# The q and k projections of two head groups by seven block products instead of eight, with v and the attended heads kept in DRAM

## The chip, the cores and the metric

One core of a Trainium2 chip runs the whole program. The metric is the device time of one execution in microseconds (us). The engines are named as in the profile: PE (TensorE matmul), PEld (its weight loads), DVE (VectorE), ACT (ScalarE), POOL (GpSimd, whose queue also issues some DMAs), SP (SyncE, which issues most loads). Each engine works through its own list of instructions in order.

## The reference

One layer of an encoder with 512 positions and 1024 channels, everything in float32:

```python
n = rms_norm(h, norm_mix_pre)
proj = n @ w_in                      # columns: u, v of the gMLP | q | k | v of attention | gates
z_gmlp, q, k, v, gates = split(proj)
y_a = u * (W_s LN(v) + b_s)          # chunked gMLP gating
q, k = partial_rope(q), partial_rope(k)          # 12 heads of 128: 3 groups of 4
for g, (window, dilation) in enumerate(((128, 1), (512, 4), (2048, 16))):
    o_g, lse_g = dilated_window_attention(q_g, k_g, v_g, dilation, ...)
y_b = sum(softmax(lse over groups) * o_g)        # 4 heads of 128
merged = sigmoid(g_a) * (y_a @ w_branch_a) + sigmoid(g_b) * (y_b @ w_branch_b)
h = h + rms_norm(merged @ w_out)
h = h + rms_norm(relu(rms_norm(h) @ w_up) ** 2 @ w_down)
```

## The kernel before, in words

Each float32 operand of a large product is split into two parts, a rounded `hi` and the rest `lo`: ACT copies to `hi`, DVE subtracts to get `lo` (`wsplit`, lines 74 and 75, for weights; `split_into`, lines 79 and 80). A product is then three matmuls, hi·hi, hi·lo and lo·hi (`mm3`, lines 84 to 86).

The stages in order of time: norm of x and the first v group; v of the two other groups (`token_major`); the q/k stage, head by head; the gMLP's v and u with head 3's attention between them (the u stage); gates and branches; w_out; up projection; down projection. `n` is kept transposed as `nh`, `nl` (128 partitions x 8 blocks x 512 positions) for the first five.

*The q/k stage* (`project_qk`) loads for each head and each of three groups one `qkw` tile (q and k weights, 512 KB together, issued by SP), splits each half, and makes q and k with one `feature_tile` each: 8 blocks x 3 matmuls of 512 columns. ACT evacuates the accumulator twice, 32 rows into `st` for the rotary step and all rows into the tile. `rotate` (lines 311 to 316) turns `st` on DVE and ACT writes it back; `split_qk` and `scores_a` make scores of group 0 (psa), `scores_b` those of groups 1 and 2 (psb); `softmax_tile` and `mix` finish the probabilities. `attend(h - 1)` runs between groups 1 and 2 of head h; head 3's runs in pieces inside the u stage. `v0h`, `v0l` and `v12` (v of all heads, 32 KB in each partition) and `ybh`, `ybl` (the attended heads, split) stay on chip throughout.

*The seven-product scheme* is already used in the gate stage (`seven`, `product`, `seven_pairs`, lines 548 to 596) and in another form in the up projection. Two output tiles of 128 columns over 512 positions are a 2 x 2 block problem: channels even/odd, positions in halves `A` and `B` of 256. Instead of eight block products there are seven, numbered 1 to 7, each 4 blocks x 3 matmuls of 256 columns. They need sums of weight blocks (tile `s`, three DVE instructions, `seven`) and sums of blocks of n. These four sums are made once by `four_sums` after the second v group, stored to DRAM (`sums`), and loaded again before the gate stage (tiles `nt`, line 635, POOL queue). Three accumulators Y, Z, X are shared by the seven products, so snapshots have to be taken between them:

```python
product(6, Y, ...)
product(1, X, ...)
nc.scalar.activation(p1, X, AF.Copy)                       # L578
nc.vector.tensor_tensor(u2, Y, p1, op=ALU.add)             # L579
product(5, Z, ...)
nc.scalar.activation(z5, Z, AF.Copy)                       # L581
product(2, X, ...); evac(i, c1[:, A], X)
product(7, Y, ...)
nc.vector.scalar_tensor_tensor(u3, Y, -1.0, p1, ...)       # L585
product(3, Z, ...)
nc.vector.tensor_tensor(c1[:, B], Z, u2, op=ALU.add)       # L587
nc.vector.tensor_tensor(c2[:, B], u3, z5, op=ALU.subtract) # L588
```

Product 4, into Y, and the last quarter (`c2[:, A]`, L592) are held back in `tail` and issued after product 6 of the next pair.

The order of instructions on each engine is set when the program is built, by a scheduler that works through the code above by its own estimate of time; pools with a number of buffers (`bufs`) say how far a producer may run ahead. Weights come from `wpool` (`raw`, `hi` and `lo` with three buffers each), accumulators from `psA` (tag `acc` four buffers, `S` two, `T` and `y` one).

Of the kernel before, what the change touches and what calls it, by code (L numbers as in the profile page):

```python
# [10 lines left out]
F32 = mybir.dt.float32  # L11
# [5 lines left out]
P = 128  # L17
# [19 lines left out]
def block_kernel(ctx: ExitStack, tc: tile.TileContext, x, norm_mix_pre, w_in, b_gate, ln_v_gain, ln_v_bias,  # L37
# [70 lines left out]

    front = ExitStack()
# [101 lines left out]
    for i in range(4):  # L211
        if i + 1 < 4:
            _, hi, lo = norm_x(blocks[i + 1], xts[i + 1], rs[i + 1])
        if i == 0:
            with tc.issue_after(hi.ins):
                for j in (2, 3):
                    rs[j], _ = square_x(blocks[j], xts[j])
        b = blocks[i]
        pv = psA.tile([P, GW], F32, name="pv", tag="acc", bufs=4)
        for k in range(KD):  # L220
            sl = slice(b * P, (b + 1) * P)
            mm3(pv, (nh[:, k, sl], nl[:, k, sl]), w0[k], k == 0, k == KD - 1)
        split_into(v0h[:, b], v0l[:, b], pv)
    start.close()

    carry = pool(right, "carry", side="right")
    ybh = carry.tile([P, NH, S], F32R, name="ybh")
    ybl = carry.tile([P, NH, S], F32R, name="ybl")
# [22 lines left out]
    sums = {n: tc.dram_tile([P, 2, KH, 256], F32R, name=f"sum{n}") for n in (6, 5, 7, 4)}  # L251

    def four_sums():
        with ExitStack() as st:
            spool = pool(st, "spool")
            f = spool.tile([P, KD, S], F32, name="nf")
# [12 lines left out]
    for g in range(2):  # L269
        def ev(r, ps, g=g):  # L270
            if r % 2:
                nc.vector.tensor_copy(v12[:, g, r], ps)
            else:
                nc.scalar.activation(v12[:, g, r], ps, AF.Copy)
        with tc.issue_after(hi.ins), tc.issue_after(lo.ins):
            token_major(COL_VV + (g + 1) * GW, lambda n, k, r: n[:, k, ROT + r:ROT + S:4], ev)
        if g == 0:
            four_sums()

# [9 lines left out]
    ppool = pool(attn, "ppool", bufs=16)  # L289
# [17 lines left out]

    def rotate(st, tiles, r0):
# [9 lines left out]
    def project_qk(h):  # L318
        got, tiles, r0 = {}, [], 0
        st = apool.tile([P, S], F32, name="st", bufs=2)  # L320
        for g in range(3):
            if g == 2:
                st, tiles, r0 = apool.tile([P, S], F32, name="st", bufs=2), [], 64
                if h:
                    attend(h - 1)
            hd0 = (g * NH + h) * HD
            raw = wload([2, KD, P], lambda r: [(r[:, 0], fcols(w_in, COL_Q + hd0, KD, P)), (r[:, 1], fcols(w_in, COL_K + hd0, KD, P))], "qkw")
            for j, nm in enumerate("qk"):
                wh, wl = wsplit(raw[:, j])
                ps = feature_tile(wh, wl, KD, nhn, nln)  # L330
                d = apool.tile([P, S], F32, name=f"{nm}{g}")
                view = ps.rearrange("p (l r) -> p r l", r=4) if g else ps
                i = r0 + 32 * len(tiles)
                for dst, src in ((st[i:i + 32], view[0:32]), (d, view)):
                    nc.scalar.activation(dst.rearrange("p (r l) -> p r l", r=4) if g else dst, src, AF.Copy)
                tiles.append(d)
                got[nm, g] = d.rearrange("p (r l) -> p r l", r=4)
# [64 lines left out]
    def mix(h):  # L402
# [4 lines left out]
        pp = psA.tile(shape, F32, name="pp", tag="T")  # L407
# [22 lines left out]
        pc = psA.tile(sq, F32, name="pc", tag="T")  # L430
# [14 lines left out]
    def attend_steps(h, tag="T", nb=1):  # L445
        hs = slice(h * HD, (h + 1) * HD)
# [30 lines left out]
        for k in range(4):  # L477
# [7 lines left out]
            a = (v0h[:, k, hs], v0l[:, k, hs])  # L485
# [6 lines left out]
        for r in range(4):  # L492
            o = py[:, r:S:4]
            for g in range(2):
                nc.tensor.matmul(o, v12[:, g, r, hs], ptb[r // 2][:, r % 2, g], start=False,  # L495
                                 stop=(r == 3 and g == 1), skip_group_check=True)
        split_into(ybh[:, h], ybl[:, h], py)
# [5 lines left out]

    yapool = pool(right, "yapool", side="right")
# [43 lines left out]
    def seven(raw, sums, split2, split1):  # L548
        raw = raw.rearrange("p (j h) (r c) -> p j (h r) c", h=2, r=2)
        s = sums()  # L550
        nc.vector.tensor_tensor(s[:, :, 0:4:2], raw[:, :, 1:3], raw[:, :, 0:1].to_broadcast([P, KH, 2, P]), op=ALU.add)
        nc.vector.tensor_tensor(s[:, :, 3], s[:, :, 2], raw[:, :, 1], op=ALU.add)
        s12 = split2(s[:, :, 2:4])
        ar = [split1(raw[:, :, 1], "ar0"), split1(raw[:, :, 2], "ar1")]
        a12 = split1(raw[:, :, 3], "a12")
        nc.vector.tensor_tensor(s[:, :, 1], s[:, :, 3], raw[:, :, 3], op=ALU.add)
        s34 = split2(s[:, :, 0:2])
        pick = lambda g, i: [z[:, :, i] for z in g]
        return {1: ar[0], 2: a12, 3: pick(s34, 1), 4: ar[1], 5: pick(s12, 0), 6: pick(s12, 1), 7: pick(s34, 0)}

    def product(n, ps, w, moving, first):
        (wh, wl), (bh, bl) = w[n], moving[n]
        for j in range(KH):
            for i, (a, b) in enumerate(((wh, bh), (wh, bl), (wl, bh))):
                nc.tensor.matmul(ps, a[:, j], b[:, j], start=first and not (j or i), stop=(j == KH - 1 and i == 2), skip_group_check=True)  # L565

    def seven_pairs(n, weights, moving, banks, snap, two, rows, evac, after):
        tail = None
        for i in range(n):
            c2, c1 = rows(i)  # L570
            w = weights(i)
            Y, Z, X = banks()
            product(6, Y, w, moving, True)
            if tail:
                tail()
            product(1, X, w, moving, True)
            p1, z5, u2, u3 = snap("p1", two), snap("z5", 1), snap("u2", 1), snap("u3", 1)
            nc.scalar.activation(p1, X, AF.Copy)  # L578
            nc.vector.tensor_tensor(u2, Y, p1, op=ALU.add)  # L579
            product(5, Z, w, moving, True)  # L580
            nc.scalar.activation(z5, Z, AF.Copy)  # L581
            product(2, X, w, moving, False)
            evac(i, c1[:, A], X)
            product(7, Y, w, moving, False)
            nc.vector.scalar_tensor_tensor(u3, Y, -1.0, p1, op0=ALU.mult, op1=ALU.subtract)  # L585
            product(3, Z, w, moving, False)
            nc.vector.tensor_tensor(c1[:, B], Z, u2, op=ALU.add)  # L587
            nc.vector.tensor_tensor(c2[:, B], u3, z5, op=ALU.subtract)  # L588

            def tail(i=i, w=w, Y=Y, p1=p1, c2=c2):  # L590
                product(4, Y, w, moving, False)
                nc.vector.scalar_tensor_tensor(c2[:, A], Y, -1.0, p1, op0=ALU.mult, op1=ALU.subtract)  # L592
                after(i)
        tail()

    steps = attend_steps(NH - 1, "S", 2)
    next(steps)
    for g2 in range(2):
        raw = wload([KD, 2 * P], lambda r: [(r, fcols(w_in, COL_U + g2 * 2 * P, KD, 2 * P))], "uw")
        for j in range(2):  # L600
# [17 lines left out]
            t = gpool.tile([P, 4, P], F32, name="sv", bufs=2)  # L618
# [11 lines left out]
    spacer(gp, 32, "tedge", "left")  # L630
    tpool = pool(gp, "tpool", bufs=4)
    nmov = {}
    for n in (6, 5, 7, 4):
        hl = tpool.tile([P, 2, KH, 256], F32R, name="nt")
        nc.gpsimd.dma_start(hl, sums[n])
        nmov[n] = (hl[:, 0], hl[:, 1])
    gst.close()
    spacer(gp, 224, "gedge", "left")
# [18 lines left out]
    def gate_weights(i):  # L657
        raw = gate_raw(i + GSTD)

        def split1(src, tag):  # L660
            hl = gapool.tile([P, 2, KH, P], F32R, name=tag)
            split_into(hl[:, 0], hl[:, 1], src)
            return hl[:, 0], hl[:, 1]

        return seven(raw.rearrange("p k r c -> p k (r c)"), lambda: wpool.tile([P, KH, 4, P], F32, name="s", tag="raw"), wsplit, split1)
# [25 lines left out]
    for d in range(GSTD):  # L691
# [5 lines left out]
        if d == 0:  # L697
            for n, (kh, half) in {1: (0, A), 2: (1, A), 3: (1, B)}.items():
                nmov[n] = (nhn[:, kh:KD:2, half], nln[:, kh:KD:2, half])
# [323 lines left out]
```

## Time and profile before

| | |
|---|---|
| median of 3 executions | 814.74 us (814.69 to 815.55) |
| the profiled execution, whole | 814.79 us |
| its span, first to last instruction | 813.0 us |
| granted TensorE clock | 0.998 |
| busy PE / PEld / DVE / ACT / POOL | 801.5 / 711.2 / 493.4 / 413.2 / 43.7 us |
| moved by DMA | 95.73 MB |

How to read the views. The page gives busy time by engine. The view of waits has "engine line waited for: us in total, times, longest". The view of stretches gives, for a piece of the span, its length, then busy time and number of instructions of each engine, the clock, the DMA engines' share and GB/s. The groups of instructions give "line engine op out<-in forms xcount | busy us, mean ns | idle before them <- releaser". The chain in order of time gives "start, us, engine, tile, line, count", and the timeline "start, us, engine, line, instruction". DMA issues give size in KB and median us from issue to landing. Buffer numbers are left out of names: `pf` is a feature tile's accumulator, `pgacc` and `pgS` those of the gate stage, `pacc` and `ptp` those of the up projection.

### The profile page before, as it was taken

The numbers are of one execution on the slowest core, as the hardware profiler recorded it, in microseconds if no ns is written. First come the engines' busy times: TensorE is split into PE (matmuls) and PEld (weight loads), VectorE is DVE, ScalarE is ACT, GpSimd is POOL, SyncE is SP. The second block draws the span as 40 slices with busy tenths as digits, with TensorE's granted clock in tenths as the row PEclk, the third lists the DMA queues.
The fourth block names the chain that finished last, engine by engine and source line by source line (L and its number), as shares of the span: only waits on it lengthen the run. The fifth ranks groups of instructions, "written<-read, shape, count | busy, mean of one in ns | idle before, by whom it ended". The sixth has DMA issues, their size and how long they took to land.

```text
span 813.0 us, 11561 instructions
## 1 busy us (share of the span) xinstructions
PE 801.5 (99%) x4629; PEld 711.2 (87%) x4629; DVE 493.4 (61%) x827; ACT 413.2 (51%) x689; POOL 43.7 (5%) x69
## 2 busy tenths in 40 slices
PE   8999999999999999999999999999999999999996
PEld 5899888888888889999988899999999888888885
DVE  6762264646463978788656479988887533333324
ACT  6341367666665555454535447666676522332212
POOL 3012000000002400000001100000000000000000
PEclk9999999999999999999999999999999999999999
DMA  9377333131312463344447222333334632332202
GB/s 309 109 242 204 87 103 104 53 102 54 97 60 65 127 209 105 79 117 118 130 140 246 80 79 87 121 105 104 105 108 144 233 112 103 104 103 75 82 1 104
DMA packets 84056, 95.73 MB, mean 118 GB/s; under 512 B 2417, under 2 KB 70033, under 8 KB 82978
## 3 DMA queue, kind: packets, MB, share of 16 engines
q1 hardware_dynamic: 80208, 77.60, 31.5%
q0 software_dynamic: 3792, 17.39, 6.2%
q8 instruction: 36, 0.59, 0.3%
q14 instruction: 18, 0.15, 0.1%
q10 hardware_dynamic: 2, 0.00, 0.0%
HBM read 86.60 MB, written 8.39 MB: 117 GB/s over the span
## 4 chain that ended last, share of the span: by engine, by line
PE 93%; DVE 3%; DMA 1%; ACT 1%; issue 0%; DVEq 0%; POOLq 0%; POOL 0%; ACTq 0%
PE pacc L890 11%; PE pd L84 9%; PE pd L85 9%; PE pd L86 9%; PE pf L85 9%; PE pf L84 9%; PE pf L86 9%; PE pgacc L565 6%; PE ptp L890 4%; PE pv L85 3%; PE pv L86 3%; PE pv L84 3%; PE pgS L565 2%; PE psb L383 1%; PE py L495 1%; DMA upw<-in_w_up_dram 1%
## 5 line engine op out<-in xcount | busy, mean ns | idle before, releaser
L84 PE MATMUL pf<-nh,hi 128*128 128x512 f32 x240 | 94.7, 395 | 0.0
L86 PE MATMUL pf<-nh,lo 128*128 128x512 f32 x240 | 94.4, 393 | 0.0
L85 PE MATMUL pf<-nl,hi 128*128 128x512 f32 x240 | 94.2, 393 | 0.0
L85 PE MATMUL pd<-hl,hh 128*128 128x512 f32 x224 | 87.2, 390 | 0.0
L84 PE MATMUL pd<-hl,hh 128*128 128x512 f32 x224 | 86.3, 389 | 0.0
L86 PE MATMUL pd<-hl 128*128 128x512 f32 x224 | 86.1, 389 | 0.0
L890 PE MATMUL pacc<-nt,hl 128*128 128x256 f32 x504 | 67.6, 280 | 0.1
L80 DVE TENSOR_TENSOR hl<-hid,hh 128x512 fp32r<-128x512 f32 x28 | 19.2, 692 | 75.6 <-ACT hh L79 75.6
L75 DVE TENSOR_TENSOR lo<-qkw,hi 128x1024 fp32r<-128x1024 f32 x24 | 29.4, 1226 | 57.7 <-ACT hi L74 57.7
L890 PEld LDWEIGHTS pacc<-nt,hl 128*128 128x128 f32 x504 | 62.7, 188 | 0.3 <-ACT hl L79 0.3
L79 ACT ACTIVATE hh<-hid 128x512 fp32r<-128x512 f32 x28 | 17.4, 630 | 89.0 <-PE pd L85 89.0
L86 PEld LDWEIGHTS pf<-nh,lo 128*128 128x128 f32 x240 | 45.1, 188 | 9.1
L85 PEld LDWEIGHTS pf<-nl,hi 128*128 128x128 f32 x240 | 45.2, 188 | 8.9
L84 PEld LDWEIGHTS pf<-nh,hi 128*128 128x128 f32 x240 | 45.2, 188 | 8.6
L86 PEld LDWEIGHTS pd<-hl 128*128 128x128 f32 x224 | 42.1, 188 | 8.7
L85 PEld LDWEIGHTS pd<-hl,hh 128*128 128x128 f32 x224 | 42.1, 188 | 8.6
L84 PEld LDWEIGHTS pd<-hl,hh 128*128 128x128 f32 x224 | 42.0, 188 | 8.6
L80 DVE TENSOR_TENSOR hl<-dnw,hl 128x1024 fp32r<-128x1024 f32 x32 | 39.1, 1225 | 13.9 <-ACT hl L79 13.9
L890 PE MATMUL pacc<-n,hl 128*128 128x256 f32 x336 | 45.2, 280 | 0.5 <-ACT z L915 0.5
L79 ACT ACTIVATE hl<-s 128x1024 fp32r<-128x1024 f32 x28 | 29.6, 1058 | 28.9 <-DVE s L874 10.6
L890 PEld LDWEIGHTS pacc<-n,hl 128*128 128x128 f32 x336 | 41.9, 188 | 0.8 <-ACT z L915 0.7
L79 ACT ACTIVATE hl<-dnw 128x1024 fp32r<-128x1024 f32 x32 | 33.4, 1048 | 12.4 <-PE pacc L890 7.5
(315 smaller groups left out, 1930.5 us busy)
## 6 DMA issues: line engine op xcount, KB each, us to landing
upw<-in_w_up_dram SPq DMA_DIRECT2D x16, 1024.0 KB, 5.5
dnw<-in_w_down_dram SPq DMA_DIRECT2D x16, 1024.0 KB, 4.9
qkw<-in_w_in_dram SPq DMA_DIRECT2D x24, 512.0 KB, 5.3
gw<-in_w_in_dram SPq DMA_DIRECT2D x16, 512.0 KB, 5.2
slab<-in_w_in_dram SPq DMA_DIRECT2D x6, 1024.0 KB, 9.2
sum<-sum POOLq DMA_DIRECT2D x4, 1024.0 KB, 7.8
nt<-sum POOLq DMA_DIRECT2D x4, 1024.0 KB, 7.5
wow<-in_w_out_dram SPq DMA_DIRECT2D x4, 1024.0 KB, 5.1
```

Source lines behind the costliest of these rows:

```text
L75: (sub or nc.vector).tensor_tensor(lo, raw, hi.bitcast(F32), op=ALU.subtract)
L79: nc.scalar.activation(hi, src, AF.Copy)
L80: return nc.vector.tensor_tensor(lo, src, hi.bitcast(F32), op=ALU.subtract)
L84: nc.tensor.matmul(ps, ah, bh, start=start, stop=False)
L85: nc.tensor.matmul(ps, ah, bl, start=False, stop=False)
L86: return nc.tensor.matmul(ps, al, bh, start=False, stop=stop)
L383: nc.tensor.matmul(ps[:, rr, g - 1], got["q", g][:, r], got["k", g][:, r], start=True, stop=True)
L495: nc.tensor.matmul(o, v12[:, g, r, hs], ptb[r // 2][:, r % 2, g], start=False, stop=(r == 3 and g == 1), skip_group_check=True)
L565: nc.tensor.matmul(ps, a[:, j], b[:, j], start=first and not (j or i), stop=(j == KH - 1 and i == 2), skip_group_check=True)
L890: nc.tensor.matmul(ps, a[:, j], b[:, j], start=first and not (j or m), stop=(j == KH - 1 and m == 2), skip_group_check=True)
```

## The change

q and k of groups 0 and 1 of every head are made as one pair by the seven-product scheme (`seven_qk`); group 2's two tiles stay with `feature_tile`. The four sums of n go straight into tiles `nmov` that stay on chip to the end of the gate stage (32 KB a partition); they are no longer stored and loaded. To make room v is split or copied into staging tiles and stored to DRAM by POOL's queue (`v0d`, `v12d`), and each head's part is loaded before it is needed into one buffer (`load_v`: for head 0 at the start, for the others after `attend(h - 1)`). The attended heads 0 to 2 are stored (`ybd`) and loaded together after the q/k stage; head 3's is written in place. Smaller: `ppool` has 15 buffers instead of 16, `sv` one instead of two, head 3's `mix` uses the accumulators tagged `S`.

```diff
+    spool = pool(right, "spool", bufs=4, side="right")
+    nmov = {n: spool.tile([P, 2, KD // 2, 256], F32R, name="nt") for n in (6, 5, 7, 4)}
...
-    vpool = pool(attn, "vpool")
-    v0h = vpool.tile([P, 4, GW], F32R, name="v0h")
-    v0l = vpool.tile([P, 4, GW], F32R, name="v0l")
-    v12 = vpool.tile([P, 2, 4, GW], F32, name="v12")
+    vtmp = pool(vst, "vtmp")
+    v0d = tc.dram_tile([P, 2, 4, GW], F32R, name="v0d")
+    v12d = tc.dram_tile([P, 2, 4, GW], F32, name="v12d")
+    ybd = tc.dram_tile([P, NH - 1, 2, S], F32R, name="ybd")
...
-        split_into(v0h[:, b], v0l[:, b], pv)
+        t = vtmp.tile([P, 2, GW], F32R, name="v0", bufs=2)
+        split_into(t[:, 0], t[:, 1], pv)
+        nc.gpsimd.dma_start(v0d[:, :, b], t)
...
-                hl = spool.tile([P, 2, KH, 256], F32R, name="sum", bufs=4)
+                hl = nmov[n]
                 split_into(hl[:, 0], hl[:, 1], part)
-                nc.gpsimd.dma_start(sums[n], hl)
...
+            t = vtmp.tile([P, GW], F32, name="v12", bufs=4)
...
+            nc.gpsimd.dma_start(v12d[:, g, r], t)
...
+    def load_v(h):
+        hs = slice(h * HD, (h + 1) * HD)
+        v0, v12 = vpool.tile([P, 2, 4, HD], F32R, name="v0s"), vpool.tile([P, 2, 4, HD], F32, name="v12s")
+        for src, dst in ((v0d, v0), (v12d, v12)):
+            nc.gpsimd.dma_start(dst.rearrange("p a b c -> p (a b) c"), src[:, :, :, hs].rearrange("p a b c -> p (a b) c"))
+        heads[h] = v0, v12
...
+    qkpool = pool(proj, "qkpool")
...
+    def seven_qk(raw, g, c2, c1):
+        w = seven(raw.rearrange("p k r c -> p k (r c)"), wsum, wsplit, split1)
+        Y, Z, X = [psA.tile([P, 512], F32, name="pg", tag="acc", bufs=4)[:, A] for _ in range(3)]
...
+        p1, z5, u2, u3 = snap("p1"), snap("z5"), snap("u2"), snap("u3")
+        product(6, Y, w, nmov, True)
+        product(1, X, w, nmov, True)
+        nc.scalar.activation(p1, view(X), AF.Copy)
+        nc.vector.tensor_tensor(u2, view(Y), p1, op=ALU.add)
+        product(5, Z, w, nmov, True)
+        nc.scalar.activation(z5, view(Z), AF.Copy)
+        product(2, X, w, nmov, False)
+        nc.scalar.activation(half(c1, 0), view(X), AF.Copy)
+        product(7, Y, w, nmov, False)
+        nc.vector.scalar_tensor_tensor(u3, view(Y), -1.0, p1, op0=ALU.mult, op1=ALU.subtract)
+        product(3, Z, w, nmov, False)
+        nc.vector.tensor_tensor(half(c1, 1), view(Z), u2, op=ALU.add)
+        nc.vector.tensor_tensor(half(c2, 1), u3, z5, op=ALU.subtract)
+        product(4, Y, w, nmov, False)
+        nc.vector.scalar_tensor_tensor(half(c2, 0), view(Y), -1.0, p1, op0=ALU.mult, op1=ALU.subtract)
...
+        load_v(h) if not h else None
...
                 if h:
                     attend(h - 1)
+                    load_v(h)
...
+            if g < 2:
+                seven_qk(raw, g, *pair)
...
+                if g < 2:
+                    nc.scalar.activation(st[i:i + 32], d[0:32], AF.Copy)
+                else:
+                    ps = feature_tile(*wsplit(raw[:, :, j]), KD, nhn, nln)
...
+        if h == NH - 1:
+            split_into(carry[0][:, h], carry[1][:, h], py)
+        else:
+            t = ypool.tile([P, 2, S], F32R, name="yb")
+            split_into(t[:, 0], t[:, 1], py)
+            nc.gpsimd.dma_start(ybd[:, h], t)
...
+    for z in range(2):
+        nc.gpsimd.dma_start(carry[z][:, :NH - 1], ybd[:, :, z])
...
-        nc.gpsimd.dma_start(hl, sums[n])
```

Where it moves instructions: on DVE before, in the q/k stage, head 1 between the rotary step and the splits of q and k (`lo` belongs to the weight splits, `ptal` to head 0's attention):

```order
L75 TENSOR_TENSOR lo<-qkw,hi 128x1024
L311 STREAM_SHUFFLE sw<-st 128x512
L312 TENSOR_TENSOR st<-st,rope 128x512
L313 TENSOR_TENSOR sw<-sw,rope 128x512
L314 TENSOR_TENSOR st<-st,sw 128x512
L80 TENSOR_TENSOR ptal<-pt,ptah 128x512
L75 TENSOR_TENSOR lo<-qkw,hi 128x1024
L80 TENSOR_TENSOR q0l<-q_1057,q0h 128x512
L80 TENSOR_TENSOR k0l<-k_1089,k0h 128x512
L80 TENSOR_TENSOR ptal<-pt,ptah 128x512
```

The same place on DVE now, where head 1's splits of q and k stand among the evacuations of head 2's first pair (`u_1730` is its u2, `u_1731` its u3, `q_1702` and `k_1703` its tiles) and the weight splits of its second (`ar_1838`, `a_1844`):

```order
L400 TENSOR_TENSOR u_1730<-pg,p_1728 128x256
L80 TENSOR_TENSOR ar_1838<-qkw,ar_1838 128x512
L80 TENSOR_TENSOR q0l<-q_1186,q0h 128x512
L80 TENSOR_TENSOR ptal<-pt,ptah 128x512
L75 TENSOR_TENSOR lo<-s,hi 128x1024
L406 SCALAR_TENSOR_TENSOR u_1731<-pg,p_1728 128x256
L80 TENSOR_TENSOR k0l<-k_1187,k0h 128x512
L409 TENSOR_TENSOR q_1702<-u_1731,z_1729 128x256
L80 TENSOR_TENSOR a_1844<-qkw,a_1844 128x512
L470 CAST k0l<-k0l 128x64 x2
L408 TENSOR_TENSOR k_1703<-pg,u_1730 128x256
```

Five evacuations a pair now stand in DVE's queue, each between splits that belong to other heads and tiles. On PE, at the end of that pair, between product 3 and product 4 (`ar_1714`) and after it:

```order
L570 MATMUL pt<-ident,p 128x128 x4
L601 MATMUL py<-ptal,v0s 128x2x128
L602 MATMUL py<-ptah,v0s 128x2x128
L600 MATMUL py<-ptah,v0s 128x256
L601 MATMUL py<-ptal,v0s 128x256
L602 MATMUL py<-ptah,v0s 128x256
L343 MATMUL pg<-nt,ar_1714 128x256 x12
L84 MATMUL psa<-k0h,q0h 128x256 x2
```

Before, PE had rows of feature tiles there; now product 4 of the pair follows product 3 with only head 0's attention between. On POOL before, from the last constants to the reload of the sums:

```order
L304 DMA wsp<-in_w_spatial_dram 128x4x128
L75 TENSOR_TENSOR lo<-uw,hi 128x1024
L510 DMA sbias<-in_b_spatial_dram 128x512
L101 MEMSET gedge 128x56
L75 TENSOR_TENSOR lo<-uw,hi 128x1024 x2
L96 TENSOR_TENSOR rs_out<-rs_in,neghalf 128x1 x2
L75 TENSOR_TENSOR lo<-uw,hi 128x1024
```

And on POOL now, from head 0's attended tile to head 3's v:

```order
L614 DMA ybd<-yb 128x1024
L305 DMA v0s<-v0d 128x8x128
L305 DMA v12s<-v12d 128x8x128
L614 DMA ybd<-yb 128x1024
L75 TENSOR_TENSOR lo<-uw,hi 128x1024 x2
L305 DMA v0s<-v0d 128x8x128
L75 TENSOR_TENSOR lo<-uw,hi 128x1024
L633 DMA sbias<-in_b_spatial_dram 128x512
L305 DMA v12s<-v12d 128x8x128
L614 DMA ybd<-yb 128x1024
```

Head 3's two loads (the last two rows that read v0d and v12d) now stand behind splits of the u weights `uw` in POOL's queue.

More of the change, by code (lines that the diff above doesn't have):

```diff
@@ L250, in block_kernel @@
     nhn, nln = nh[:, :, nat], nl[:, :, nat]
-    sums = {n: tc.dram_tile([P, 2, KH, 256], F32R, name=f"sum{n}") for n in (6, 5, 7, 4)}
     def four_sums():
         with ExitStack() as st:
-            spool = pool(st, "spool")
-            f = spool.tile([P, KD, S], F32, name="nf")
+            f = pool(st, "fpool").tile([P, KD, S], F32, name="nf")
             for k in range(0, KD, 2):
@@ L278, in block_kernel @@
             four_sums()
+    vst.close()
     def feature_tile(wh, wl, nk, mh, ml, tag="acc"):
@@ L306, in block_kernel, with seven @@
     by_c = perm[:, 2 * P + 4:2 * P + 8].unsqueeze(1).unsqueeze(3)
+    def seven(raw, sums, split2, split1):
+        raw = raw.rearrange("p (j h) (r c) -> p j (h r) c", h=2, r=2)
+        s = sums()
+        nc.vector.tensor_tensor(s[:, :, 0:4:2], raw[:, :, 1:3], raw[:, :, 0:1].to_broadcast([P, KH, 2, P]), op=ALU.add)
+        nc.vector.tensor_tensor(s[:, :, 3], s[:, :, 2], raw[:, :, 1], op=ALU.add)
+        s12 = split2(s[:, :, 2:4])
+        ar = [split1(raw[:, :, 1], "ar0"), split1(raw[:, :, 2], "ar1")]
+        a12 = split1(raw[:, :, 3], "a12")
+        nc.vector.tensor_tensor(s[:, :, 1], s[:, :, 3], raw[:, :, 3], op=ALU.add)
+        s34 = split2(s[:, :, 0:2])
+        pick = lambda g, i: [z[:, :, i] for z in g]
+        return {1: ar[0], 2: a12, 3: pick(s34, 1), 4: ar[1], 5: pick(s12, 0), 6: pick(s12, 1), 7: pick(s34, 0)}
@@ new lines, in product, with seven_pairs, tail @@
+    def product(n, ps, w, moving, first):
+        (wh, wl), (bh, bl) = w[n], moving[n]
+        for j in range(KH):
+            for i, (a, b) in enumerate(((wh, bh), (wh, bl), (wl, bh))):
+                nc.tensor.matmul(ps, a[:, j], b[:, j], start=first and not (j or i), stop=(j == KH - 1 and i == 2), skip_group_check=True)
+    def seven_pairs(n, weights, moving, banks, snap, two, rows, evac, after):
+        tail = None
+        for i in range(n):
+            c2, c1 = rows(i)
+            w = weights(i)
+            Y, Z, X = banks()
+            product(6, Y, w, moving, True)
+            if tail:
+                tail()
+            product(1, X, w, moving, True)
+            p1, z5, u2, u3 = snap("p1", two), snap("z5", 1), snap("u2", 1), snap("u3", 1)
+            nc.scalar.activation(p1, X, AF.Copy)
+            nc.vector.tensor_tensor(u2, Y, p1, op=ALU.add)
+            product(5, Z, w, moving, True)
+            nc.scalar.activation(z5, Z, AF.Copy)
+            product(2, X, w, moving, False)
+            evac(i, c1[:, A], X)
+            product(7, Y, w, moving, False)
+            nc.vector.scalar_tensor_tensor(u3, Y, -1.0, p1, op0=ALU.mult, op1=ALU.subtract)
+            product(3, Z, w, moving, False)
+            nc.vector.tensor_tensor(c1[:, B], Z, u2, op=ALU.add)
+            nc.vector.tensor_tensor(c2[:, B], u3, z5, op=ALU.subtract)
+            def tail(i=i, w=w, Y=Y, p1=p1, c2=c2):
+                product(4, Y, w, moving, False)
+                nc.vector.scalar_tensor_tensor(c2[:, A], Y, -1.0, p1, op0=ALU.mult, op1=ALU.subtract)
+                after(i)
+        tail()
@@ L546, in block_kernel @@
     token_major(COL_V, lambda n, k, c: n[:, k, ROT + c * P:ROT + (c + 1) * P], evac_v)
[L548 to L594, printed above, removed]
@@ L658, in gate_weights @@
         raw = gate_raw(i + GSTD)
[L660 to L665, printed above, removed]
+        return seven(raw.rearrange("p k r c -> p k (r c)"), wsum, wsplit, lambda src, tag: split1(src, tag, gapool))
     def gate_banks():
```

76 lines of the change are left out of this document (44 added, 32 removed).

## The prediction

> **What bounds the kernel now.** I read the page's busy times first, then who waits for whom on TensorE (PE), then the stretches by stage, then the chain in order of time where one form of product stands beside the other, and last the groups by form for prices.
>
> ```profile
> span 813.0 us, 11561 instructions
> PE 801.5 (99%) x4629; PEld 711.2 (87%) x4629; DVE 493.4 (61%) x827; ACT 413.2 (51%) x689; POOL 43.7 (5%) x69
> ...
> PE 93%; DVE 3%; DMA 1%; ACT 1%; issue 0%; DVEq 0%; POOLq 0%; POOL 0%; ACTq 0%
> ...
> PE idle L153 <- DVE onesq L59: 1.1, 1, 1.1
> PE prs L530 <- ACT wst L528: 0.7, 1, 0.7
> ...
> PE pd L84 <- DVE gs L592: 0.5, 1, 0.5
> ```
>
> PE is the bound from end to end: 93% of the chain that ended last, and no wait of PE longer than 1.1 us. Time is gained only by giving PE less to do, and is lost wherever PE then has to wait. The stretches:
>
> ```profile
> core 0: us, PE busy (x) PEld busy (x) DVE busy (x) ACT busy (x) POOL busy (x), PEclk, DMA share, GB/s
> 163.85:205.40 41.55, 41.55 (x223) 35.51 (x222) 21.88 (x63) 28.70 (x59) 0.00 (x0) 1.00 0.27 76
> 205.40:246.94 41.54, 41.54 (x222) 35.50 (x222) 21.86 (x63) 28.22 (x57) 0.00 (x0) 1.00 0.25 77
> 265.00:300.00 35.00, 34.31 (x187) 28.98 (x186) 30.39 (x53) 16.55 (x26) 9.16 (x11) 1.00 0.60 195
> 343.60:359.05 15.45, 15.45 (x110) 14.47 (x110) 12.23 (x20) 7.72 (x13) 0.00 (x0) 1.00 0.40 103
> ```
>
> Rows one and two are one head each of the q/k stage: 41.55 us, PE never idle, VectorE (DVE) busy 53%, ScalarE (ACT) 69%. Row four is one gate tile pair, the stage that already uses the seven-product scheme: PE never idle there either, DVE at 79%, ACT at 50%. Row three is the u stage: DVE at 87%, and PE loses 0.69 us, the wait for wst above.
>
> **PE's saving.** One pair of q and k tiles is now two `feature_tile` calls, 48 matmuls of 512 columns; it becomes seven products of 12 matmuls of 256 columns, 84 in all. A matmul's own duration (395 and 280 ns in the groups) is no price, since they overlap; the distance between starts is.
>
> ```profile
> 151.11 0.40 PE L84 MATMUL pf<-nh,hi 128*128 128x512 f32 x1
> ...
> 155.43 0.40 PE L85 MATMUL pf<-nl,hi 128*128 128x512 f32 x1
> ...
> 359.05 1.40 PE pgacc L565 x12
> 361.83 1.43 PE pgS L565 x12
> 363.26 2.83 PE pgacc L565 x24
> 366.10 1.44 PE pgS L565 x12
> 367.53 2.85 PE pgacc L565 x24
> 539.80 4.20 PE pacc L890 x36
> ```
>
> The first two are the first and last of 20 matmuls in a row: 4.32 us over 19 steps, 0.2274 us each, so 48 take 10.92 us. The next five are one gate pair's seven products in the chain: 9.95 us for 84. The saving is 0.97 us a pair; two of three head groups by four heads are 8 pairs: **7.8 us off PE**. (At the up projection's pace, last row, 0.1167 us a matmul, 84 take 9.80 and the saving is 9.0 us; the same operand layout speaks for the gate's pace.)
>
> **What DVE and ACT get in return.** Prices by form:
>
> ```profile
> L75 DVE TENSOR_TENSOR lo<-qkw,hi 128x1024 fp32r<-128x1024 f32 x18 | 22.1, 1226 | 37.7 <-ACT hi L74 37.7
> L80 DVE TENSOR_TENSOR ar<-gw,ar 128x512 fp32r<-128x512 f32 x14 | 9.6, 687 | 2.7 <-ACT ar L79 2.7
> L551 DVE TENSOR_TENSOR s<-gw 128x1024 f32<-128x1024 f32 x6 | 7.3, 1222 | 3.1 <-DMA gw<-in_w_in_dram 3.1
> L552 DVE TENSOR_TENSOR s<-s,gw 128x512 f32<-128x512 f32 x6 | 4.1, 682 | 0.0
> L579 DVE TENSOR_TENSOR u<-pgacc,p 128x256 f32<-128x256 f32 x7 | 2.9, 418 | 0.0
> L79 ACT ACTIVATE ar<-gw 128x512 fp32r<-128x512 f32 x14 | 8.7, 628 | 11.2 <-PE pgacc L565 11.2
> L578 ACT ACTIVATE p<-pgS 128x256 f32<-128x256 f32 x7 | 2.7, 384 | 5.3 <-PE pgS L565 5.3
> L335 ACT ACTIVATE q<-pf 128x512 f32<-128x512 f32 x10 | 5.9, 590 | 0.1
> ...
> 347.63 0.68 DVE L80 TENSOR_TENSOR b<-bw,b 128x512 fp32r<-128x512 f32 x1
> 348.23 0.69 DVE L688 TENSOR_TENSOR gs<-gs 128x512 f32<-128x512 f32 x1
> ```
>
> Per pair DVE loses 2 splits of 1024 columns (2.45 us) and gets as many back for the sums (2.45), plus three splits of 512 (ar0, ar1, a12: 2.06), the sums themselves (1.22 + 2 x 0.68 = 2.59) and five evacuations of 256 (u2, u3, three halves: 2.09): +6.74 us in durations. The last two rows show neighbours that start 0.60 apart and last 0.68, so the 11 instructions more cost some 0.08 less each: +5.9. Per head that is +11.7 to +13.5 on 21.9, **33.6 to 35.4 us of DVE** in a head that PE now does in 41.55 - 1.95 = 39.6: 85 to 89%. ACT gets three splits (1.88) and three copies of 256 (1.15) and loses two evacuations (1.18), the 32-row copies staying: +1.9 a pair, 32.2 us a head, 81%. Neither becomes the bound by its sum; both stand nearer to PE than before, and DVE and ACT run in order.
>
> Inside a pair PE now depends on them at short range: product 2 reuses the bank that p1 is copied from, 7 follows u2, 3 follows z5, 4 follows u3. In the gate stage product 4 is put behind product 6 of the next pair (`tail`); here it comes right behind product 3, one product (1.4 us) after the one that u3 reads, unless the order puts other matmuls between, as it does in many places. The wait that this may bring is shown by no row. Its ends: nothing, as in the gate stage (PE 15.45 of 15.45); and one 128x1024 DVE instruction of 1.23 us in front of u3 and one in front of z5's consumer, 2.45 us a pair, 19.6 us in all. The u stage is the nearest row by load: DVE at 87%, PE idle 0.69 of 35.0, 2.0%. On four heads of 39.6 us that is **3.1 us, 0.39 a pair**, which I take.
>
> Weights can't be the late ones: ar0, ar1, a12 have one buffer each, freed by their product in the pair before and needed a pair (9.95 us) later less one or two products, some 8.5 us for ACT and DVE work of 1.3 us; `hi` and `lo` have three buffers, as now.
>
> **Sums and v.** Leaving the four sums on chip removes 4 stores and 4 loads of 1 MB. v, stored in 12 pieces and reloaded head by head (8 loads of 512 KB), and three heads' yb add back some 11 MB. None is on the chain now, and the DMA engines are busy 0.25 to 0.27 there. POOL issues these:
>
> ```profile
> nt<-sum POOLq DMA_DIRECT2D x4, 1024.0 KB, 7.5
> h<-h2d POOLq DMA_DIRECT2D x4, 512.0 KB, 4.3
> ...
> DMA to landing us min/median/max: 6.5/8.4/10.4
> ...
> 254.69 2.39 POOL L75 TENSOR_TENSOR lo<-uw,hi 128x1024 fp32r<-128x1024 f32 x1 [188.46 <-ACT hi L74]
> ...
> 246.04 0.89 PE py L495 x8
> ```
>
> Heads 1 and 2 have most of a head between `attend` of the head before, which frees the one v buffer, and their own. Only head 3 is near: by the order PE does 19 + 24 matmuls of 512 (9.8 us) and about 25 small ones (0.11 us each by the last row, 2.8 us) between the last use of head 2's v0 and the first of head 3's, 12.6 us, while POOL may still be at a split of uw (2.4 us) and the load takes 4.3 us (512 KB) to 10.4 (the slowest nt). 12.8 against 12.6 at worst: cost 0. v's evacuations write staging tiles in place of kept ones, same sizes; a staging tile is reused two blocks (some 11 us) or a whole projection later: 0. The new load layout of qkw moves the same rows. One p buffer and one sv buffer less, the S bank for head 3's mix: DVE passes them in order anyway, 0. The gate stage, the up and the down projection keep their instructions: 0.
>
> The Trainium skill, page "SBUF — State Buffer", section on the three doors ("DVE blocks DMA"), says that a DMA issued by GpSimd waits for its descriptors while VectorE holds the shared port, and gives a case five times longer (620 to 3100 ns). By that, v's reload beside a DVE at 85% could take 5 x 4.3 = 21.5 us, an estimate. The nt transfers above, twice as large, ran beside a DVE at 87% (the third stretch) and took 6.5 to 10.4 us, so the trace bears little of it out. It is rival E.
>
> **The sum.** 814.79 (the profiled execution: span 813.0 and 1.79 around it; the median shown is 814.74, the same) - 7.8 + 3.1 = **810.1 us**.
>
> **Rivals.**
> B, all hidden: PE waits nowhere, as in the gate stage: 814.8 - 7.8 = 807.0, or 805.8 at the up projection's pace. For it: 15.45 of 15.45 at DVE 79%. Against: DVE and ACT both above 80% here, product 4 close behind.
> C, the wait eats the gain: 0.8 to 1.15 us a pair, half to a whole 1.23 us instruction in front of u3: 813.3 to 816.2.
> D, slower: the in-order DVE becomes the bound inside the pairs. The rotation (four instructions of 0.69), softmax and mix of a head stand in the same queue; when u3 or z5's consumer is behind such a run, PE stands, and nothing fills since g2's tiles were used up. From 0.97 us a pair on it is a loss; one 1.23 and one 0.42 instruction, 1.65 a pair, give 814.8 + 8 x 0.68 = 820.2. Against: in all stages shown the order kept PE fed.
> E, head 3's v late by the shared port: 21.5 + 2.4 - 12.6 = 11 us at most, 821; half of it 815.5.
>
> Chances: forecast A (wait 0.1 to 0.7 us a pair, 807.7 to 812.5) 0.42; B 0.22; C 0.14; D 0.17; E 0.05. No difference means within 0.2% (813.1 to 816.4), about what a measurement of this kernel tells from no change: faster A + B and a little of E, 0.65; same C and some of E, 0.16; slower 0.19. The range goes from B's lower end, 805.5, into D, 817.5.
>
> **What the profile after would show.** PE's groups with 672 matmuls of 128x256 at the seven products' line L343 in the q/k stage and 384 fewer of 128x512; a chain with 9.95 us for 84 of them where nothing is mixed in; heads 39.6 to 40.4 us apart (psb to psb); DVE busy 33 to 36 us a head, ACT 32; PE's waits there for DVE u and the c halves (L400, L406, L408, L411) or ACT z (L402), 3 us in all; no PE wait at py for v0s or v12s. Wrong it would be if heads come 41 us apart or more with PE waiting on DVE (D), if they come at 39.6 (B), if the 256-wide matmuls are not 0.118 us apart here, or if py waits for a DMA (E).

## The result: 810.35 us, and the profile after

| kernel | median us (executions) | ratio to before, 95% interval |
|---|---|---|
| before | 814.82 (814.69 to 815.55; 4) | |
| changed | 810.35 (808.92 to 810.89; 4) | 0.9941 [0.9923, 0.9958] |
| changed, run again (`again`) | 809.86 (809.78 to 809.98) | 0.9938 [0.9925, 0.9950] |

The change saves 4.5 to 5.0 us. The profiled execution took 810.79 us. Its page (span, busy times, the chain that ended last by engine):

```profile
span 809.0 us, 12339 instructions
...
PE 795.8 (98%) x4917; PEld 720.3 (89%) x4917; DVE 539.1 (67%) x915; ACT 423.3 (52%) x721; POOL 57.0 (7%) x86
...
PE 92%; DVE 3%; ACT 2%; DMA 1%; issue 1%; POOL 0%; DVEq 0%; POOLq 0%; ACTq 0%
```

PE still bounds the kernel. DVE has 45.7 us more than before, 5.7 for each of 8 pairs, ACT 10.1, 1.3 a pair. PE's waits (engine, line, waited for: us in total, times, longest; `p` is the snapshot p1, `vln` the gMLP's normed v, `ptal` and `ptb` are turned probabilities, and below `wst` are the turned spatial weights and `prs` their sums):

```profile
PE pg L343 <- ACT p L399: 1.3, 1, 1.3
PE idle L159 <- DVE onesq L59: 1.1, 1, 1.1
PE pg L692 <- DVE vln L667: 0.9, 1, 0.9
...
PE pt L583 <- DVE ptal L80: 0.4, 1, 0.4
...
PE py L607 <- ACT ptb L585: 0.2, 1, 0.2
```

Four of these lie in the q/k and u stages, 2.8 us together; each occurs once. The stages, from one stage's first matmul to the next's, the last one to its last matmul (us, told apart in the traces by the tiles that they write; turn is the first part of the up projection, in which w_out's result is turned; each row is one profiled execution):

| kernel | v | q/k and u | gate | w_out | turn | up | down |
|---|---|---|---|---|---|---|---|
| before | 45.1 | 226.7 | 114.3 | 45.5 | 24.4 | 133.8 | 179.5 |
| changed | 45.1 | 221.8 | 114.3 | 45.5 | 24.4 | 134.8 | 179.5 |
| again | 45.1 | 221.8 | 114.3 | 45.5 | 24.4 | 133.8 | 179.5 |

All of the gain lies in q/k and u: 4.9 us. The up projection, which the change doesn't touch, took 1.0 us more in the profiled execution, and not when the same program ran again. The chain in order of time, the same group in changed and then in again:

```profile
535.09 4.24 PE pacc L949 x36
```

```profile
534.91 4.20 PE pacc L949 x36
```

0.1178 against 0.1167 us a matmul, one program. Six of the 14 profiles of this study have an up projection of 134.8, the others 133.8 or 133.9: a difference of 1 us between two executions says nothing on a change unless the stage shows it. So I read stages.

### The profile page after: what moved, and what is told of

The parts are those of the page before. It is cut to its first block, busy times and chain, and to the rows that moved or that the text cites. A ratio compares the mean times of both kernels' runs of the same rounds, so it can differ in the third digit from the quotient of the medians.

```text
span 809.0 us, 12339 instructions
## 1 busy us (share of the span) xinstructions
PE 795.8 (98%) x4917; PEld 720.3 (89%) x4917; DVE 539.1 (67%) x915; ACT 423.3 (52%) x721; POOL 57.0 (7%) x86
## 4 chain that ended last, share of the span: by engine, by line
PE 92%; DVE 3%; ACT 2%; DMA 1%; issue 1%; POOL 0%; DVEq 0%; POOLq 0%; ACTq 0%
PE pacc L949 11%; PE pg L343 9%; PE pd L86 9%; PE pd L84 9%; PE pd L85 9%; PE pgacc L343 6%; PE pf L84 5%; PE pf L85 5%; PE pf L86 5%; PE ptp L949 4%; PE pv L85 4%; PE pv L86 3%; PE pv L84 3%; PE pgS L343 2%; PE psb L494 1%; PE py L607 1%
## 5 line engine op out<-in xcount | busy, mean ns | idle before, releaser
L84 PE MATMUL pf<-nh,hi 128*128 128x512 f32 x112 | 44.6, 398 | 0.0
L74 ACT ACTIVATE hi<-s 128x1024 fp32r<-128x1024 f32 x30 | 31.7, 1059 | 24.7 <-DVE s L330 11.3
L85 PE MATMUL pf<-nl,hi 128*128 128x512 f32 x112 | 44.0, 393 | 0.0
L86 PE MATMUL pf<-nh,lo 128*128 128x512 f32 x112 | 43.9, 392 | 0.0
L75 DVE TENSOR_TENSOR lo<-s,hi 128x1024 fp32r<-128x1024 f32 x30 | 36.6, 1224 | 9.7 <-ACT hi L74 9.6
L80 DVE TENSOR_TENSOR hl<-s,hl 128x1024 fp32r<-128x1024 f32 x28 | 34.2, 1222 | 6.4 <-ACT hl L79 6.2
L85 PE MATMUL pv<-lo,nh 128*128 128x512 f32 x96 | 38.2, 397 | 0.0
```

The costliest lines, as they stand in the source:

```text
L74: nc.scalar.activation(hi, raw, AF.Copy)
L75: (sub or nc.vector).tensor_tensor(lo, raw, hi.bitcast(F32), op=ALU.subtract)
L80: return nc.vector.tensor_tensor(lo, src, hi.bitcast(F32), op=ALU.subtract)
L84: nc.tensor.matmul(ps, ah, bh, start=start, stop=False)
L85: nc.tensor.matmul(ps, ah, bl, start=False, stop=False)
L86: return nc.tensor.matmul(ps, al, bh, start=False, stop=stop)
```

## The experiments

The main account is one table. The ideal is the q/k and u stage of the kernel without any seven-product pair (225.8, `none` below) less 0.97 us a pair; idle is the stage's length less PE's busy time; slow clock is what the granted clock below 1 took, summed over slices of 2 us; rest is what then remains of the stage. Part of the rest belongs to the waits: a matmul of 512 columns lasts 0.39 us in these traces and the next one starts after 0.23, so a wait costs some 0.16 us more than PE's idle time.

| kernel | pairs | median us | ratio [95%] | q/k and u | ideal | idle | slow clock | rest | gate |
|---|---|---|---|---|---|---|---|---|---|
| none | 0 | 813.21 | 0.9978 [0.9969, 0.9987] | 225.8 | 225.8 | 0 | 0 | 0 | 113.6 |
| g0_only | 4 | 808.95 | 0.9932 [0.9920, 0.9944] | 221.8 | 221.9 | 0 | 0 | -0.1 | 113.6 |
| g1_only | 4 | 812.65 | 0.9974 [0.9965, 0.9984] | 225.4 | 221.9 | 1.4 | 1.7 | 0.4 | 113.6 |
| changed | 8 | 810.35 | 0.9941 [0.9923, 0.9958] | 221.8 | 218.0 | 2.8 | 0 | 1.0 | 114.3 |
| all3 | 12 | 829.77 | 1.0180 [1.0166, 1.0194] | 241.3 | 214.2 | 17.0 | 5.1 | 5.0 | 114.3 |
| pool1 | 8 | 814.72 | 0.9996 [0.9987, 1.0005] | 227.5 | 218.0 | 5.9 | 1.7 | 1.9 | 113.6 |
| p1dve | 8 | 808.72 | 0.9922 [0.9909, 0.9934] | 219.6 | 218.0 | 1.3 | 0 | 0.3 | 114.3 |
| uwdve | 8 | 811.26 | 0.9959 [0.9946, 0.9972] | 224.4 | 218.0 | 4.0 | 1.7 | 0.7 | 113.6 |
| gbank | 8 | 809.99 | 0.9932 [0.9919, 0.9946] | 221.8 | 218.0 | 2.8 | 0 | 1.0 | 113.6 |
| p1_gbank | 8 | 807.02 | 0.9900 [0.9886, 0.9913] | 219.6 | 218.0 | 1.3 | 0 | 0.3 | 113.6 |
| p1_gbank_early | 8 | 806.86 | 0.9899 [0.9885, 0.9912] | 219.6 | 218.0 | 1.1 | 0 | 0.5 | 113.6 |
| g1_early | 4 | 816.72 | 1.0018 [1.0010, 1.0027] | 228.3 | 221.9 | 4.6 | 1.7 | 0.1 | 113.6 |

**The changed kernel again, and parts of the change.** Four kernels differ only in which groups go by seven products; `again` is the changed kernel as it is. The edit in short: both tests of the group change, and a feature tile of group 0 is copied as in the kernel before.

```diff
-            if g < 2:
+            if g in GROUPS:     # none: (); g0_only: (0,); g1_only: (1,); all3: (0, 1, 2)
```

*again.* 

> The changed kernel once more, unaltered. Theory (7.8 us less PE work, about 2 us of new waits, the rest spread): 810 to 811 us. Its up projection took 1 us longer in the profiled execution than before's, at the same instructions; if that belongs to the execution, another profile shows 0.1167 us between its matmuls (4.20 us for 36) in some executions and 0.1178 (4.24) in others; if it belongs to the program, always 0.1178.

*none.* 

> All else of the change (v and attended heads through DRAM, the sums kept on chip, the pools), but q and k of all groups by feature tiles of 512 columns. Theory: the passages through DRAM cost nothing, 814.2 to 815.4. Rival (reloads late, or POOL and DVE in each other's way): over 816.

*g1_only.* 

> Only group 1 by seven products (4 pairs), group 0 as before. Theory (a pair saves 0.97 us of PE, waits come only where DVE is loaded over 85%): nearly all of 3.9 us is kept, 811.0 to 811.8. Rival (each pair loses a fixed 0.4 us by its own short chain): 812.5.

*all3.* 

> All three groups by seven products (12 pairs), no feature tile left in the q/k stage. DVE gets 21.9 + 3 x 5.7 = 39 us a head against PE's 41.55 - 2.9 = 38.6. Theory (DVE's load decides): DVE becomes the bound, waits of some us a head, 810 to 820. Rival (the order keeps PE fed whatever the load): 4 x 0.97 us less than the changed kernel, 806.5.

`again` gave 809.86, just under its 810 to 811: the gain repeats. `none` missed both expectations: all the rest of the change together doesn't cost nothing, it brings 1.7 us (813.21 against 814.88 of the kernel before in those rounds). The stretch of its q/k and u stage (length, then busy time and instructions of PE, PEld, DVE, ACT, POOL, clock, DMA share, GB/s):

```profile
81.80:307.60 225.80, 225.80 (x1161) 191.54 (x1160) 126.04 (x310) 141.22 (x271) 24.44 (x25) 1.00 0.42 114
```

PE is never idle: the 0.69 us wait for wst has gone, and 0.3 us more. The gate stage is 0.7 us shorter; `gbank` below says why.

`all3` is 14.9 us slower than before, 10 us above the upper end of its theory. Some of PE's waits in its q/k and u stage:

```profile
PE pg L692 <- DVE vln L667: 3.5, 1, 3.5
PE pg L343 <- DVE lo L75: 2.2, 3, 1.0
PE pg L343 <- DVE u L406: 2.2, 4, 1.1
PE pg L343 <- ACT hi L74: 2.0, 2, 1.6
PE pg L343 <- ACT z L402: 1.9, 3, 1.3
```

Here are the waits in front of u3 (L406) and z5 (L402) that the prediction priced, on DVE and ACT alike. Of these rows the changed kernel has only the wait for vln, 0.9 us there. DVE is not the bound by its load: from 81.8 to 241.8 us it is busy 133.8 of 160.0 us, ACT 112.1. That PE waits because no feature tile is left to fill it between the products of a pair fits, but was not shown.

`g1_only` puzzled: 0.56 us below `none` where 3.9 would be the pairs' worth. That is near its rival's 812.5, a fixed loss in each pair; the trace, further down, shows something else.

**Group 0 alone.** 

> Only group 0's pair of each head goes by seven products (4 pairs instead of 8); groups 1 and 2 by feature tiles. Ideal: 4 x 0.97 = 3.9 us below the kernel without any (813.2), so 809.3. Theory 1 (the pairs' prices add up: group 1 alone gained 0.56 of 3.9, both together 3.3, so group 0's share is 2.8): 810.4, 810.0 to 811.0, and the last v accumulator starts 4 us earlier than without. Theory 2 (any group alone gains little, since the gain of a pair is eaten where the next feature tile's weights or accumulators are not ready, and only both together pay): 812.3 to 813.2.

808.95: its four pairs bring 4.0 us of stage, all of the ideal, PE never idle. `g0_only`, then the changed kernel:

```profile
81.70:303.50 221.80, 221.80 (x1305) 195.47 (x1304) 145.95 (x348) 145.27 (x284) 24.93 (x25) 1.00 0.42 116
```

```profile
81.70:303.53 221.83, 218.99 (x1449) 199.31 (x1447) 165.89 (x389) 150.09 (x300) 24.27 (x25) 1.00 0.44 121
```

The changed kernel's stage, with twice the pairs, is just as long (221.8 us), and the intervals of the two times overlap. So in the change as it stands group 1's four pairs, another 3.9 us off PE, brought nothing net: the waits that came with them took 3.8 us back.

Both theories were wrong on the time, theory 1 because it took `g1_only`'s loss for a price of pairs. The trace of `g1_only` shows what it was. PE's timeline at one place in the u stage, then stretches:

```profile
268.00 0.38 PE L600 MATMUL py<-ptah,v0s 128*128 128x256 f32 x1 [0.32 <-ACT ptah L79]
269.46 2.08 PE L653 MATMUL prs<-wst,onesq 128*128 128x512 f32 x2 [1.08 <-ACT wst L651]
```

```profile
268.00:270.00 2.00, 0.92 (x2) 0.69 (x3) 2.00 (x7) 1.92 (x4) 1.45 (x2) 0.87 0.14 49
270.00:272.00 2.00, 2.00 (x6) 0.90 (x5) 2.00 (x4) 0.63 (x1) 0.77 (x2) 0.50 0.01 4
272.00:274.00 2.00, 2.00 (x15) 2.00 (x14) 2.00 (x7) 0.74 (x2) 0.32 (x1) 0.78 0.00 0
```

PE waits 0.32 and 1.08 us for ACT, and then the granted clock is 0.50 for some 3.4 us: 2 x (0.13 + 0.50 + 0.22) = 1.7 us lost behind waits of 1.4 in all. The prs matmuls take 2.08 us here; in `p1dve`, at full clock, 1.13:

```profile
267.93 1.13 PE L653 MATMUL prs<-wst,onesq 128*128 128x512 f32 x2 [0.69 <-ACT wst L651]
```

Idle and clock take 3.1 of the missing 3.5 us. The Trainium skill, page "TensorE: Matmul & The Clock Gate", Part 1, gives two clock states, full and half, judged over windows of some 3.4 us. The 0.50 and its 3.4 us agree; that waits of 0.32 and 1.08 us, 0.4 us apart, were enough, where the page's table speaks of an idle window, is this trace's.

**That group 1's pairs are good, tried by moving the wait away.** The spatial weights are turned ahead of the gMLP's v projection.

```diff
+    spatial_turn()          # the five transposes, the copies to cols and wst
     token_major(COL_V, ...)
...
-            ps = feature_tile(*wsplit(raw[:, :, 1 - br]), KD, nhn, nln)
+            ps = feature_tile(*wsplit(raw[:, :, 1 - br]), KD, nhn, nln, "S")
```

*g1_early.* 

> Only group 1's pairs by seven products, as in g1_only, with the spatial weights turned ahead of the gMLP's v projection (and the gate's first tiles tagged S, so that its last bank stays free as in g1_only). Theory 1 (group 1's pairs gain as much as group 0's; g1_only lost it in one place of the u stage, a 1.1 us wait of PE for wst with some 3 us of halved clock behind it, together some 2.7 us): 809.7 to 810.3, no stretch with a clock under 0.99. Theory 2 (the pairs of group 1 themselves bring little, by their strided copies and the rotation behind them): 811.6 to 812.7.

816.72, 6 us above theory 1 and 4 above theory 2: in the new order PE meets two other waits, in head 3's mix and at the turned weights.

```profile
PE pc L543 <- DVE xc L541: 2.9, 1, 2.9
PE pv L84 <- ACT wst L651: 1.7, 1, 1.7
```

Idle 4.6, slow clock 1.7, and what is left is 0.1 us from the ideal. So in both kernels with group 1 alone the account leaves the pairs their full gain; a kernel that has group 1's pairs and neither wait was not found, so this is read from traces, not shown by a run.

**DVE unloaded.** Three splits of a pair go to POOL.

```diff
-        split_into(hl[:, 0], hl[:, 1], src)
+        nc.scalar.activation(hl[:, 0], src, AF.Copy)
+        (nc.gpsimd if pl is qkpool else nc.vector).tensor_tensor(hl[:, 1], src, hl[:, 0].bitcast(F32), op=ALU.subtract)
```

*pool1.* 

> The three 512-column splits (lo of ar0, ar1, a12) of the q/k pairs are done by POOL instead of DVE: 24 x 0.69 = 16.5 us less on DVE, some 24 x 1.2 = 29 us more on POOL, which stands idle there. Theory 1 (DVE's full queue makes the small gaps of the pairs, 2 to 3 us of the 8 pairs in all): 807.5 to 809.0, DVE some 522 us busy. Theory 2 (what PE waits for there is ACT's queue, and DVE has slack): 809.7 to 810.6, the same as the changed kernel, with the 1.3 us wait for p at L399 still there. Rival 3 (POOL beside DVE slows DVE down, or lo comes too late from POOL): above 811.

814.72 (813.1 to 817.2 in 12 executions, the profiled one 815.9), the rival. Groups by form, `pool1` first, then the changed kernel:

```profile
L379 POOL TENSOR_TENSOR ar<-qkw,ar 128x512 fp32r<-128x512 f32 x14 | 19.7, 1409 | 68.8 <-ACT ar L378 62.4 <-PE pf L85 6.3
...
L330 DVE TENSOR_TENSOR s<-s,qkw 128x512 f32<-128x512 f32 x6 | 7.1, 1181 | 0.0
```

```profile
L80 DVE TENSOR_TENSOR ar<-qkw,ar 128x512 fp32r<-128x512 f32 x14 | 9.5, 688 | 1.4 <-ACT ar L79 1.2
...
L330 DVE TENSOR_TENSOR s<-s,qkw 128x512 f32<-128x512 f32 x6 | 4.1, 684 | 0.0
```

A split takes POOL 1.41 us where DVE takes 0.69, and the pairs' sum of line 330 on DVE takes 1.18 instead of 0.68: DVE's total falls by 5.1 us (539.1 to 534.0) where 16.5 were taken off. The Trainium skill, page "SBUF — State Buffer", section "SBUF: two separate sides", says that the two engines share a port pair by an exclusive lock, also where a DVE instruction has two SBUF inputs and the GpSimd one reads SBUF; the lengthened sums have two SBUF inputs, and agree; u2, with one input from the accumulator `pg`, takes 0.42 us in both kernels. PE's stage got 5.7 us longer, with a 2.4 us wait for vln and the half clock behind it among it.

**The 1.3 us wait for p1.** The chain in order of time, changed kernel, ACT's part ahead of that wait:

```profile
186.78 0.59 ACT st L446
...
187.39 0.60 ACT k L446
187.99 0.95 ACT hi L74
188.94 0.51 ACT q L421
...
189.47 0.63 ACT k L421
...
190.13 1.72 ACT p L551 x4
...
191.86 0.63 ACT q L421
...
192.50 0.64 ACT k L421
...
193.16 0.63 ACT q0h L79
193.78 0.28 ACT p L399
...
194.11 4.53 PE pg L343 x36
```

Seven microseconds of other work, without a gap, stand ahead of p1 in ACT's in-order queue: evacuations and a weight split, write-backs of the rotary step, the scaling of probabilities.

```diff
-        nc.scalar.activation(p1, view(X), AF.Copy)
+        nc.vector.tensor_copy(p1, view(X))
```

*p1dve.* 

> p1 of the q/k pairs is copied by DVE instead of ACT (8 copies of 128x256, some 0.35 us each). Theory 1 (the 1.3 us wait of PE for p1 of head 3's first pair comes from seven microseconds of other work ahead of it in ACT's queue, and u2 no longer waits for another engine): 808.4 to 809.2, no wait for p at L399. Rival (p1 now stands behind DVE's 1.2 us splits and sums, DVE being the busier engine): 810.0 to 812.0, with new waits of PE for DVE p at L399.

808.72, theory 1. The intervals of this time and the changed kernel's overlap, so I go by the stage: 219.6, 2.2 us less. The rows for p at L399 and for vln are gone, and the longest waits there are now:

```profile
PE prs L653 <- ACT wst L651: 0.7, 1, 0.7
...
PE psa L84 <- ACT k0h L468: 0.6, 1, 0.6
```

So 2.2 of the 3.8 us that the changed kernel's pairs lost hung on one copy's engine, the order that followed from it included; the wait for p1 was 1.3 of it. DVE, the busier of the two engines in all, was the better place. Whether p1 ahead of other work in ACT's queue would do as much was not tried.

**The 0.9 us wait for vln.** The chain, changed kernel:

```profile
265.32 2.38 POOL lo L75
267.73 1.22 DVE s L329
268.95 0.61 DVE st L663
...
270.06 0.55 DVE vln L667
270.75 0.46 PE pg L692 x2
```

The first gate pair's sum (s) takes a `wpool` buffer that POOL's last split of uw frees, and stands ahead of vln's steps in DVE's queue.

```diff
-            wh, wl = wsplit(raw[:, :, j * P:(j + 1) * P], sub=nc.gpsimd)
+            wh, wl = wsplit(raw[:, :, j * P:(j + 1) * P], sub=nc.vector)
```

*uwdve.* 

> The lo parts of the u weights are made by DVE instead of POOL (4 x 1.23 us more on DVE, 4 x 2.4 less on POOL). Theory 1 (the 0.9 us wait of PE for vln came from the chain: lo of the last uw on POOL, late in its queue, frees the buffer of the first gate pair's sum on DVE, which stands ahead of vln): 808.9 to 809.4, no wait for vln above 0.3 us. Rival (DVE at 83 to 87% has no room for them in the u stage: the wait stays or moves to another tile): 809.8 to 811.5.

811.26, the rival: the wait grew to 1.95 us and the clock halved behind it.

```profile
PE pg L692 <- DVE vln L667: 1.9, 1, 1.9
```

POOL was the last link, but DVE has no room for its work there: in `uwdve` the chain ahead of that vln is DVE alone from 261.5 to 271.8 us, with 0.1 us of gaps.

**The gate stage's 0.7 us.** Ends of the gate stage, PE's timeline, again and then `gbank`:

```profile
415.79 1.56 PE L343 MATMUL pgacc<-nt,ar 128*128 128x256 f32 x12
417.87 0.50 PE L84 MATMUL pd<-hi,mh 128*128 128x512 f32 x1 [0.52 <-DVE gs L370]
```

```profile
415.97 1.56 PE L343 MATMUL pgacc<-nt,ar 128*128 128x256 f32 x12
417.37 0.39 PE L84 MATMUL pd<-hi,mh 128*128 128x512 f32 x1
```

```diff
-            ps = feature_tile(*wsplit(raw[:, :, 1 - br]), KD, nhn, nln)
+            ps = feature_tile(*wsplit(raw[:, :, 1 - br]), KD, nhn, nln, "S" if br else "acc")
```

*gbank.* 

> The changed kernel with the second feature tile of the first gate pair in an accumulator tagged S instead of acc, so that the four acc banks are handed out one further in the rest of the gate stage. Theory (the first accumulator of w_out is the bank of the last pair's product 4 in before and after, and PE waits 0.5 us for DVE to empty it; in the kernels whose gate stage takes 113.5 instead of 114.3 us it is another bank): gate stage 113.5, no wait of pd for gs, 809.0 to 809.5. Rival (the 0.8 us come from elsewhere, the bank is free anyway): 809.8 to 810.9.

The trace shows the theory: the step from product 4 to pd is 1.40 instead of 2.08 us, the stage 113.6 instead of 114.3. The time, 809.99, stands in the rival's range and decides nothing, since the intervals of gbank and changed overlap; the profiled executions of both, 810.27 and 810.79, had the slower up projection (134.8). So whether w_out starts in a bank that still has to be emptied depends on how the four `acc` buffers were handed out before, and edits far away move this stage by 0.7 us. `uwdve` and `pool1` hand out as many as the changed kernel and have the short stage too, so the number alone doesn't decide; what does there was not followed.

**Together.** Two kernels combine p1 on DVE with the bank shift; the second also turns the spatial weights early (both first gate tiles tagged S).

*p1_gbank.* 

> p1 of the q/k pairs copied by DVE, and the bank shift of the gate stage. If the two gains add up: 808.7 - 0.8 = 807.9 (807.4 to 808.3). Rival (the order of instructions moves and a wait in the u stage comes back): above 808.7.

*p1_gbank_early.* 

> As p1_gbank (both feature tiles of the first gate pair tagged S), and the spatial weights are turned (five transposes and the two copies) ahead of the v projection of the gMLP instead of behind the first u tile, so that the matmul prs finds wst long ready. Theory: the 0.7 us wait of prs for wst goes as well: 806.8 to 807.6; without any wait the seven-product pairs would give 813.2 - 7.8 = 805.4. Rival (another wait in the u stage, vln or a sum of DVE, takes its place): 807.7 to 809.

807.02 and 806.86: 1.0% below before, and below the changed kernel by more than its interval. The first came out lower than the sum of the two gains (807.4 to 808.3); by stages the two gains just add up, 219.6 and 113.6. The early turn took away the wait of prs and brought one of pv for wst (0.5 us), so the two are the same within their intervals.

## Why the prediction was right, and where it was not

The forecast was 810.1; 810.35 and 809.86 were measured. Step by step:

*PE's saving, 7.8 us: right.* In the chain of the changed kernel:

```profile
112.68 11.35 PE pg L343 x96
```

0.118 us a matmul, the gate's pace, and `g0_only` got 4.0 us for four pairs (3.9 by the price).

*The waits, 3.1 us spread over the pairs: right in kind, too small, and in other places.* Idle and small gaps in q/k and u took 3.8 us, and the gate stage's end took back 0.7 that the rest of the change had freed: 4.5. It isn't 0.39 a pair. Group 0's pairs alone wait for nothing; with both groups it is a few single waits, of which the largest comes through ACT, whose order I had not followed (I had priced u3 and z5 behind DVE), and the next through POOL and DVE in the u stage, which I had taken as untouched. All eight pairs so gain 7.8 - 3.8 = 4.0 us in this stage, no more than group 0's four pairs alone. The 2.0% of the u stage, from which I scaled, gave the size by luck.

*The rest of the change at 0: wrong by 1.7 us.* The step "None is on the chain now" holds for the transfers; but the order and the banks moved with them, and that freed 1.0 us in the q/k and u stages and 0.7 in the gate stage. Which of the moved parts did the first was not tried.

So the sum is, by measured terms, 814.8 - 1.7 - 7.8 + 3.8 + 0.7 = 809.8, against 814.8 - 7.8 + 3.1 = 810.1. Two errors of 1.4 and 1.7 us nearly cancel, which is luck: that PE's saving would come was understood, where the waits would stand was not.

*DVE and ACT.* DVE 5.7 us a pair (5.9 to 6.7 forecast), ACT 1.3 (1.9). In one stretch of 36 us in the q/k stage

```profile
147.20:183.20 36.00, 36.00 (x278) 34.63 (x278) 29.73 (x79) 30.30 (x65) 2.34 (x3) 1.00 0.47 127
```

DVE is at 83% and ACT at 84%: ACT stood as near to PE as DVE. The first psb of the four heads are 34.8, 38.7 and 38.0 us apart, not 39.6 to 40.4; work moves across that mark, so it was a bad one, before too (36.6, 41.5, 41.5).

*Head 3's v.* No wait of PE for it. DMA issues (size, median us to landing):

```profile
v0s<-v0d POOLq DMA_DIRECT2D x4, 512.0 KB, 5.5
v12s<-v12d POOLq DMA_DIRECT2D x4, 512.0 KB, 5.4
```

Slower than the 4.3 taken; the slowest is head 3's v0s with 7.8, far from 21.5. The two loads inside the stretch above, with DVE at 83%, took 4.8 and 4.6 us, so rival E falls. The Trainium skill, page "SBUF — State Buffer", section "SBUF: two separate sides", ties that stall to a DVE instruction in a two-port mode, a condition that the prediction left out. (Of the kernel before, the prediction's 6.5 to 10.4 us are three of the four nt loads; all four took 5.2 to 10.4.)

*Rival D*, waits inside the pairs beyond what they save, isn't there with 8 pairs; `all3` shows it with 12, behind ACT as well as DVE.

## What to carry to other kernels

When PE is the bound and never idle, price the work taken off PE by the distance between starts; where nothing new waits it comes in full, as with group 0 alone. What is lost again are a few single waits, here as much as the second half of the change had saved. They are found by following each in-order queue (ACT and POOL as well as DVE) for what stands ahead of the instruction that PE needs soon. A short copy that PE waits for doesn't always belong on the engine with less work in all: what stands ahead of it in the queue at that moment counts, and here, by one run, DVE was better. An edit that changes the number of buffers handed out, or the order, moves stages far away by half a microsecond; run the change without its main part to see it.

## What the runs showed of the hardware that was not expected

- Behind waits of PE its granted clock fell to 0.50 for some 3.4 us, 1.7 us lost each time: in `g1_only` (waits of 0.32 and 1.08 us close together), `uwdve` (1.95), `pool1` (2.4) and `g1_early` (2.9 and 1.7 close together); `all3` lost 5.1 us in three places. The 1.28 and 0.91 us waits of the changed kernel brought no such drop. What decides was not found.
- POOL's splits beside DVE lengthened DVE's sums of two SBUF inputs (line 330) from 0.68 to 1.18 us; u2, with one input from an accumulator, stayed at 0.42.
- Matmuls of one program in the up projection came 0.1167 us apart in some executions and 0.1178 in others, 1.0 us over that stage.
